# Seven products instead of eight for pairs of channel tiles, one shared work area, and low parts made by adding transfers

## The chip, the cores and the metric

The kernel runs on one core of a Trainium2 chip. The metric is device time in microseconds (us). The kernel before took 606.78 us, the median of three runs (606.14 to 609.61). The profile comes from one execution of 606.02 us, whose span from the first to the last instruction is 604.0 us.

The engines are TensorE (PE, matrix products; PEld is its weight load), VectorE (DVE), ScalarE (ACT), GpSimd (POOL) and SyncE (SP, which only issues transfers). Each works its own queue in order.

## The reference, cut to what matters

One layer of a hybrid backbone is applied to 128 context tokens and 512 latent tokens. All 640 tokens share one input projection of 1024 x 6176 weights. Its columns feed two head groups whose outputs are joined by a 2048 x 1024 output projection.

```python
h = _rms(x, norm_pre_w) * (1 + scale) + shift        # 640 tokens x 1024
u = h @ w_in
z, xbc, dt_raw, q, k, v, g = split(u)                # 1024, 2048, 32, 512, 512, 1024, 1024 columns
xbc = silu(depthwise_conv3(xbc) + conv_b)            # xs 1024, B 512, C 512
y_s = bidirectional_scan(C, B * dt, xs, decay) + D_skip * xs        # SSD, 16 heads, chunks of 128
y_s = _rms(y_s * silu(z), ssd_norm_w)
y_r = bidirectional_scan(rope(q), rope(k), v, fixed decay)          # retention, 8 heads
y_r = groupnorm(y_r) * ret_norm_w * silu(g)
out = concat([y_s, y_r]) @ w_out
y = x + gate * _rms(out, norm_post_w)
```

The convolution runs over neighbouring tokens, separately in context and latent tokens. So xs, B, C and z are wanted with channels on partitions and tokens along the row ("channel tiles" of 128 channels x 640 tokens). V, G, Q and K are wanted with tokens on partitions.

## The kernel before, in words

Every large product is made in three passes: each fp32 operand is split into a high part (rounded to the fp32r type) and a low part (the rest), and high x high, high x low and low x high are added in PSUM. `hh` and `hl` hold the two parts of the normalised input, eight k-tiles of 128 rows by 640 tokens.

Weights come in pieces of 256 KB (128 x 512 values), in the order that `plan` lists. `load_split` (L157) gives each a `raw` buffer (4 of them), a `whi` and a `wlo` buffer (7 each). SP loads `raw`, ACT rounds it into `whi` (L174), and VectorE subtracts to get `wlo` (through the helper `tt`, L131). `feed` (L181) keeps loads up to six pieces and splits up to three pieces ahead of use; `take` hands pieces to a product.

The kernel has a start phase, four stages g = 0 to 3, and the output projection:

- Start: for each k-tile, the modulation (tiles `mod`), transposes (`tr`), ScalarE's scaling into `h32`, the split into `hh`/`hl`, and the V and G columns of stage 0 into five accumulators `acc`. The order is written out by hand in the string `START`.
- A stage runs four kinds of products. `gemm_wide` makes V and G: 512 columns wide, all five token tiles open at once, k-tile by k-tile (tile `gw`; stage 0 has its V and G from the start phase). `gemm_tok` makes Q and K: 256 or 288 columns, token tile by token tile (tile `gt`). `gemm_z` makes the two z tiles of the stage before, and `gemm_s` makes B, C and two xs tiles. Both call `gemm_ch` (tile `gc`): one channel tile is 8 k-tiles x 3 passes x 2 halves of 320 tokens = 48 matmuls in two accumulators. `ev_conv` copies the result into `u` with ScalarE and does the convolution and SiLU; `ev_z` does the SiLU of z.
- Scan work is cut into small steps that are called between matmuls. `slot()` counts positions in the product code (66 in a full stage) and calls the steps that are due: `s_steps(g)` is the SSD scan of four heads, `r_steps(p)` the retention scan of two heads, `dt_steps` the step sizes. The calls `s_job` and `job` name the first and last slot of each.
- Output: `gemm_wide` over the retention half for 2 x 512 columns, over the SSD half for 512 columns, then `gemm_out` (tile `go`) for the last 512 columns in 256-column groups, with the residual and store per token tile.

`job(...)` sets where steps stand in the program, and the framework orders each engine's queue from that when the kernel is built, with what is ready first: retention tables that are called at slot 12 stand at 44 us in the trace. PSUM has five banks for product accumulators (`pg`) and three for scan work (`pi`). Memory for stage work lies in pools: `rp` for retention, `sp_` for SSD.

Of the kernel before, what the change touches and what calls it, by code (L numbers as in the profile page):

```python
# [17 lines left out]
P = 128  # L18
D = 1024
KT = 8  # L20
T = 640
NCK = 5
# [13 lines left out]
CU, CL, CDU, CDL, CPOS, CONE, CS0, CS1, CTP = (  # L36
    0, 128, 256, 384, 512, 640, 768, 896, 1024)
CN = 1040
# [10 lines left out]
G6:34 G6:012 H7:4 F2 G7:012 G7:34  # L49
# [3 lines left out]
def plan():  # L53

    want = []
    for p in range(4):
        if p:
            vg = [(a + p * 256, a + p * 256 + 256) for a in (V0, G0)]
            want += [("w_in", [k], vg) for k in range(KT)]
        qk = [(Q0 + p * P, Q0 + (p + 1) * P), (K0 + p * P, K0 + (p + 1) * P)]  # L60
        if p == 0:
            qk.append((DT0, DT0 + 32))
        want += [("w_in", [2 * s, 2 * s + 1], qk) for s in range(4)]
        zc = [Z0 + q * 256 + e * P for q in ([p - 1] if p else []) for e in range(2)]
        sc = [B0 + p * P, C0 + p * P, XS0 + p * 256, XS0 + p * 256 + P]
        if p == 3:
            sc += [Z0 + 768, Z0 + 768 + P]
        for a in zc + sc:
            want += [("w_in", list(range(4 * s, 4 * s + 4)), [(a, a + P)]) for s in range(2)]
    for half, cb in ((1, 0), (1, 2), (0, 0)):  # L70
        want += [("w_out", [8 * half + k], [(cb * 256, cb * 256 + 512)]) for k in range(KT)]
    for cb in (2, 3):
        want += [("w_out", [2 * s, 2 * s + 1], [(cb * 256, cb * 256 + 256)]) for s in range(4)]
    return want

# [8 lines left out]
def constants():  # L84
# [5 lines left out]
        np.where(p < 64, i + 1, 128 - i), np.ones((P, P)),  # L90
        np.broadcast_to(p % 32 == 0, (P, P)), np.broadcast_to(p % 32 == 1, (P, P)),
        np.concatenate([np.broadcast_to(127 - j, (P, 8)), np.broadcast_to(j, (P, 8))], axis=1),
# [13 lines left out]
def body(ctx, tc, io):  # L106
# [15 lines left out]
    def mm(out, a, b, start, stop, big=False):  # L122
        r = pe.matmul(out, lhsT=a, rhs=b, start=start, stop=stop)  # L123
        if big:
            last["mm"] = getattr(r, "ins", r)
# [26 lines left out]

    hh = hp.tile([P, KT, T], F32R, name="hh")
    hl = hp.tile([P, KT, T], F32R, name="hl")
# [3 lines left out]
    at = np.cumsum([0] + [len(rows) * sum(b - a for a, b in ranges) for _, rows, ranges in want])  # L158

    def load_split(n):  # L160

        _, rows, ranges = want[n]
        nk, c = len(rows), sum(b - a for a, b in ranges)
        extra = n == len(want) - 1
        raw = wp.tile([P, nk, c], F32, tag="raw", name="raw", bufs=4)
        hi = (wx[0] if extra else wp).tile([P, nk, c], F32R, tag="whi", name="whi", bufs=1 if extra else 7)
        lo = (wx[0] if extra else wp).tile([P, nk, c], F32R, tag="wlo", name="wlo", bufs=1 if extra else 7)
        sp.dma_start(
            out=raw.rearrange("p k c -> p (k c)"),
            in_=io["ws"][P * int(at[n]):P * int(at[n + 1])].rearrange("(p x) -> p x", p=P),  # L170
        )

        def split():
            act.copy(hi, raw)  # L174
            tt(lo, raw, hi.bitcast(F32), ALU.subtract)
        return hi, lo, split

    wx = []
    state = {"ld": 0, "sp": 0, "use": 0}
    pieces = {}  # L180

    def feed(ahead_load=4, ahead_split=2):
        while state["ld"] < min(len(want), state["use"] + ahead_load):
            pieces[state["ld"]] = load_split(state["ld"])
            state["ld"] += 1
        while state["sp"] < min(state["ld"], state["use"] + ahead_split):
            pieces[state["sp"]][2]()
            state["sp"] += 1

    def take(n):  # L190

        feed(max(4, n), n)
        got = [pieces.pop(state["use"] + i)[:2] for i in range(n)]
        state["use"] += n
        return got
# [5 lines left out]
    def slot():  # L201
        feed(6, 3)
        clock["slot"] += 1
        while jobs and jobs[0][0] <= clock["slot"]:
            jobs.pop(0)[2]()
# [32 lines left out]
    rp = tc.alloc_tile_pool(name="rp", bufs=1, side="right")  # L238
    st_ = tc.alloc_tile_pool(name="st", bufs=1, side="right")


    xs_t = []
    wm_t, w0_t = {}, {}
# [6 lines left out]
    def load_w0(kt):  # L250
        raw = st_.tile([P, 512], F32, tag="raw0", name="raw0", bufs=3)
        sp.dma_start(out=raw, in_=io["w0"][kt])
        w0_t[kt] = raw
# [17 lines left out]
    junk = hl.rearrange("p k t -> p (k t)")[:, KT * T - D - 1:]  # L271
# [28 lines left out]
    w0 = {}  # L300

    def split0(kt):
        raw = w0_t.pop(kt)
        hi = st_.tile([P, 512], F32R, tag="w0h", name="w0h", bufs=3)
        lo = st_.tile([P, 512], F32R, tag="w0l", name="w0l", bufs=3)
        act.copy(hi, raw)
        tt(lo, raw, hi.bitcast(F32), ALU.subtract)
        w0[kt] = (hi, lo)

# [10 lines left out]
    def h_tile(kt, ts):  # L320
        ash = ash_t[kt]
        h32 = st_.tile([P, 512], F32, tag="h32", name="h32", bufs=3)[:, 0:len(ts) * P]
# [3 lines left out]
        for c, u in ((0, [t for t in ts if t == 0]), (1, [t for t in ts if t])):  # L326
            if u:
                q = slice((u[0] - ts[0]) * P, (u[-1] + 1 - ts[0]) * P)
                act.activation(h32[:, q], tr[:, q], AF.Identity,
                               bias=ash[:, c:c + 1], scale=ash[:, 2 + c:3 + c])  # L330
        q = slice(ts[0] * P, (ts[-1] + 1) * P)
        vec.tensor_copy(hh[:, kt, q], h32)
        r = tt(hl[:, kt, q], h32, hh[:, kt, q].bitcast(F32), ALU.subtract)
# [7 lines left out]
    def gemm0(kt, t):  # L341
        wh, wl = w0[kt]
        s = slice(t * P, (t + 1) * P)
        mm(acc[t], hh[:, kt, s], wh, kt == 0, False)
        mm(acc[t], hh[:, kt, s], wl, False, False)
        mm(acc[t], hl[:, kt, s], wh, False, kt == KT - 1)
# [3 lines left out]
        "M": load_wm, "W": load_w0, "L": load_x, "A": mod_a, "S": split0, "B": mod_b, "N": norm_x, "R": rest_x,  # L350
    }
    for op in START.split():
# [8 lines left out]
        elif op[0] == "F":  # L361
            feed(k, 0)
        elif op[0] == "C":
            sp.dma_start(out=cst, in_=io["cst"])
            sp.dma_start(out=rope, in_=io["rope"])
        else:
            steps[op[0]](k)
# [40 lines left out]
    for t in range(NCK):  # L408
        ev_v(0, t, acc[t][:, 0:256])
        ev_g(0, t, acc[t][:, 256:512])  # L410
    st_.release()

    sp_ = tc.alloc_tile_pool(name="sp", bufs=1, side="left")
    sqacc = sp_.tile([P, T], F32, name="sqacc")
    dtr = sp_.tile([P, NCK, 32], F32, tag="m", name="dtr", bufs=2)

    def gemm_tok(n, ev):
        ws = take(4)
        for t in range(NCK):
            ps = pg.tile([P, 512], F32, tag="g", name="gt")  # L420
            s = slice(t * P, (t + 1) * P)
            for kt in range(KT):
                wh, wl = ws[kt // 2]
                mm(ps[:, 0:n], hh[:, kt, s], wh[:, kt % 2], kt == 0, False)
                mm(ps[:, 0:n], hh[:, kt, s], wl[:, kt % 2], False, False)
                mm(ps[:, 0:n], hl[:, kt, s], wh[:, kt % 2], False, kt == KT - 1, big=True)
                if kt in (3, 7):
# [724 lines left out]
```

## Time and profile before

| | us |
|---|---|
| median of 3 runs | 606.78 |
| the profiled execution | 606.02 |
| its span | 604.0 |
| TensorE busy | 582.3 |
| VectorE busy | 418.1 |
| ScalarE busy | 337.4 |
| GpSimd busy | 31.3 |
| granted TensorE clock, mean | 0.993 |

The parts of the span, by the tile that TensorE writes: start 0 to 62.5 us; stage 0 Q/K to 78.5 and its B, C, xs to 122.3; stage 1 to 230.7; stage 2 with V/G 230.7 to 265.6, Q/K to 283.4, z, B, C, xs to 339.8; stage 3 with V/G and Q/K to 392.3 and z, B, C, xs, z to 469.7; output projection 469.7 to 597; the rest to 604.

In such rows an engine's busy time is the union of its instructions' spans. The rows of a line give the count, then the busy time of the group and the mean duration in ns of one, then the idle time ahead of them.

### The profile page before, as it was taken

What the parts mean: (1) busy time and instruction counts of PE and PEld (TensorE: products, weight loads), DVE (VectorE), ACT (ScalarE), POOL (GpSimd) and SP (SyncE); (2) the same over time, 40 slices, a digit from 0 to 9 for tenths busy, and PEclk for the clock granted to TensorE, in tenths of its full rate; (3) what the DMA queues carried; (4) which work ended last, traced back from release to release, by engine and by line L of the source; (5) the groups of instructions that cost most, each with busy time, mean ns of one, the idle gap of its engine ahead of it and who ended that gap; (6) DMA issues with size and microseconds to landing.
All of it is one profiled execution on the core that took longest, in us unless ns stands there. A gap on an engine that the chain in (4) does not pass through costs nothing.

```text
span 604.0 us, 10966 instructions
## 1 busy us (share of the span) xinstructions
PE 582.3 (96%) x3833; PEld 521.5 (86%) x3833; DVE 418.1 (69%) x942; ACT 337.4 (56%) x934; POOL 31.3 (5%) x112
## 2 busy tenths in 40 slices
PE   5899998999999999999999999999999999999995
PEld 3577998978999998889999888999999777788895
DVE  3657498855698866668897746798867866743665
ACT  5436255665667764465766646566755857262421
POOL 1000001200000010000011000000110000000010
PEclk9899999999999999999999999999999999999998
DMA  8694231553335633232554223354537777384033
GB/s 348 229 362 161 63 105 48 162 146 109 99 97 159 185 91 86 80 122 70 189 172 112 76 69 105 102 163 131 160 96 223 209 266 221 116 272 120 18 109 135
DMA packets 47638, 87.44 MB, mean 145 GB/s; under 512 B 5792, under 2 KB 18656, under 8 KB 46048
## 3 DMA queue, kind: packets, MB, share of 16 engines
q1 hardware_dynamic: 47296, 86.57, 45.2%
q8 instruction: 30, 0.49, 0.3%
q14 instruction: 24, 0.20, 0.1%
q10 hardware_dynamic: 288, 0.18, 0.1%
HBM read 75.03 MB, written 9.60 MB: 140 GB/s over the span
## 4 chain that ended last, share of the span: by engine, by line
PE 65%; DVE 13%; ACT 9%; DMA 6%; issue 5%; POOL 2%; SPq 0%; POOLq 0%; DVEq 0%; ACTq 0%
PE gw L123 24%; PE gc L123 11%; PE gt L123 9%; PE acc L123 5%; PE go L123 4%; DMA cf<-cumd 3%; PE ss L123 2%; PE mod L123 2%; DVE wlo L131 2%; DVE SC L128 2%; PE sfb L123 1%; PE ry L123 1%; POOL sm L131 1%; DVE yc L128 1%; ACT jk L733 1%
## 5 line engine op out<-in xcount | busy, mean ns | idle before, releaser
L131 DVE TENSOR_TENSOR wlo<-raw,whi 128x512 fp32r<-128x512 f32 (+1 forms) x120 | 82.2, 690 | 49.2 <-ACT whi L174 48.3
L174 ACT CAST whi<-raw 128x512 fp32r<-128x512 f32 (+1 forms) x120 | 73.6, 619 | 76.3 <-PE gw L123 46.1
L123 PE MATMUL gc<-hh,whi 128*128 128x320 f32 x384 | 96.7, 331 | 0.0
L123 PE MATMUL gc<-hl,whi 128*128 128x320 f32 x384 | 88.3, 310 | 0.0
L123 PE MATMUL gc<-hh,wlo 128*128 128x320 f32 x384 | 87.6, 309 | 0.0
L123 PEld LDWEIGHTS gc<-hh,whi 128*128 128x128 f32 x384 | 63.9, 189 | 1.1
L123 PEld LDWEIGHTS gc<-hl,whi 128*128 128x128 f32 x384 | 64.3, 188 | 0.1
L123 PEld LDWEIGHTS gc<-hh,wlo 128*128 128x128 f32 x384 | 64.1, 188 | 0.0
L123 PE MATMUL gw<-whi,hh 128*128 128x512 f32 x120 | 50.6, 421 | 0.8 <-ACT u L484 0.8
L123 PE MATMUL gw<-whi,hl 128*128 128x512 f32 x120 | 47.0, 392 | 0.0
L123 PE MATMUL gw<-wlo,hh 128*128 128x512 f32 x120 | 46.8, 390 | 0.0
L123 PE MATMUL gt<-whi,hh 128*128 128x256 f32 (+1 forms) x160 | 46.3, 289 | 0.0
L123 PE MATMUL gt<-wlo,hh 128*128 128x256 f32 (+1 forms) x160 | 45.7, 286 | 0.0
L123 PE MATMUL gt<-whi,hl 128*128 128x256 f32 (+1 forms) x160 | 45.7, 286 | 0.0
L862 ACT ACTIVATE m<-gu,dt 128x128 f32<-128x128 f32 x80 | 31.3, 391 | 16.5 <-DVE gu L131 14.6
L834 ACT ACTIVATE cf<-cf,dmc 128x128 f32<-128x128 f32 x80 | 26.5, 393 | 18.4 <-DMA cf<-cumd 18.4
L131 DVE TENSOR_TENSOR m<-m,cf 128x512 f32<-128x512 f32 x40 | 27.5, 689 | 8.8 <-ACT cf L863 8.2
L123 PE MATMUL gw<-whi,mrh 128*128 128x512 f32 x80 | 32.3, 404 | 0.0
L123 PE MATMUL gw<-wlo,mrh 128*128 128x512 f32 x80 | 31.2, 391 | 0.0
L123 PEld LDWEIGHTS gt<-whi,hh 128*128 128x128 f32 x160 | 30.5, 190 | 0.7 <-issue 0.5
L863 ACT ACTIVATE cf<-gu,dt 128x128 f32<-128x128 f32 x80 | 31.0, 387 | 0.0
L123 PE MATMUL gw<-whi,mrl 128*128 128x512 f32 x80 | 30.9, 391 | 0.0
(232 smaller groups left out, 1327.8 us busy)
## 6 DMA issues: line engine op xcount, KB each, us to landing
raw<-ws SPq DMA_DIRECT2D x116, 256.0 KB, 2.8
cf<-cumd SPq DMA_DIRECT2D x20, 512.0 KB, 4.2
wm<-wm SPq DMA_DIRECT2D x8, 1024.0 KB, 8.2
mraw<-mixd SPq DMA_DIRECT2D x16, 320.0 KB, 3.4
ef<-ecumd SPq DMA_DIRECT2D x32, 128.0 KB, 3.3
wg<-wg SPq DMA_DIRECT2D x4, 1024.0 KB, 5.9
x<-x SPq DMA_DIRECT2D x5, 512.0 KB, 7.3
mixd<-rmix SPq DMA_DIRECT2D x20, 128.0 KB, 2.7
```

The source lines that it names most:

```text
L123: r = pe.matmul(out, lhsT=a, rhs=b, start=start, stop=stop)
L128: eng.scalar_tensor_tensor(out=out, in0=in0, scalar=s, in1=in1, op0=op0, op1=op1)
L131: return eng.tensor_tensor(out=out, in0=a, in1=b, op=op)
L174: act.copy(hi, raw)
L733: act.activation(jk, yc[:, h], AF.Square, scale=P ** -0.5, accum_out=sm[:, 2 + h:3 + h])
L834: act.activation(cf[:, e, 1, q], cf[:, e, 1, q], AF.Identity, bias=dmc[:, c, h:h + 1])
L862: act.activation(m[:, e, q], gu[:, 0], AF.Copy, scale=dt[:, c, h:h + 1])
L863: act.activation(cf[:, e, 1, q], gu[:, 1], AF.Copy, scale=dt[:, c, 16 + h:17 + h])
```

## The change

Pairs. `gemm_ch` becomes `gemm_pair`: two channel tiles (B and C, the two xs, the two z) form a 2 x 2 block product (two tiles x two halves of k, two halves of k x two halves of tokens). It is made of seven products of quarters in place of eight. Each product is 4 k-tiles x 3 passes = 12 matmuls of 322 columns, 84 for a pair where 96 stood. The token row gets two zero columns after the context and two at the end (`TW` = 644), so a half is 322. The seven results are combined in three accumulators X, Y, Z, two of them added to twice or kept open after a partial read, with ScalarE copies and five VectorE instructions of 322 columns:

```python
steps = [
    (X, half(0, 0), True, lambda: act.copy(s1, X)),
    (Y, sm(0), True, lambda: tt(b0, Y, s1, ALU.add)),
    (Z, sm(3), True, None),
    (Y, sm(1), False, lambda: (tt(b1, Y, s1, ALU.add), tt(b1, Z, b1, ALU.subtract))),
    (X, half(0, 4), False, lambda: act.copy(a0, X)),
    (Y, half(1, 4), False, lambda: tt(a1, Y, s1, ALU.add)),
    (Z, sm(2), False, lambda: tt(b0, Z, b0, ALU.subtract)),
]
```

The sums of input quarters `sh`, `sl` are made once in the start phase by `sums(k)`, for k = 0 to 3: four VectorE instructions of 322 columns, then for two rows of 644 a ScalarE copy and a VectorE subtraction. `START` calls three of them as T0, T1, T2; the fourth stands after the evacuation of `acc`.

```diff
-G6:34 G6:012 H7:4 F2 G7:012 G7:34
+T0 G6:34 G6:012 T1 H7:4 F2 G7:012 T2 G7:34
...
+    def sums(k):
+        a, b, c, d = (rows[k + i][:, h * HW:(h + 1) * HW] for i in (0, 4) for h in range(2))
+        tt(d, b, d, ALU.subtract)
+        tt(b, a, b, ALU.subtract)
+        tt(a, d, a, ALU.subtract)
+        tt(c, c, a, ALU.add)
+        for i in range(2):
+            r = rows.pop(k + 4 * i)
...
+            act.copy(hi, r)
+            tt(lo, r, hi.bitcast(F32), ALU.subtract)
```

Weight pieces. A pair has seven pieces where it had four in all: three quarters as they are, two sums of two quarters that POOL makes by an adding transfer onto a loaded quarter, and two sums that VectorE adds from neighbouring pieces. The buffers are 6 `raw` and 5 `whi`/`wlo`, loads stand up to six pieces past the last split, splits up to four ahead of use. Pieces of one k-tile of w_in (V/G of stages 1 to 3, Q/K of stage 0) get their low part another way: ScalarE writes minus the high part, and a POOL transfer adds the weights from memory onto it.

```diff
+    def pair(a, b):
+        lo, hi = list(range(4)), list(range(4, 8))
+        a11, a12, a21, a22 = (("w_in", k, [(c, c + P)]) for c in (a, b) for k in (lo, hi))
+        load(*a11)
+        want.append(("sum", (-1, 2)))
+        load(*a11, a21)
+        load(*a21, a22)
+        load(*a12)
+        want.append(("sum", (-4, -1)))
+        load(*a22)
...
+            if i:
+                pool.dma_start(out=out, in_=source(n, i), accum_op=ALU.add)
+            else:
+                sp.dma_start(out=out, in_=source(n, i))
...
+        if want[n][0] == "load" and want[n][1][0][0] == "w_in" and raw.shape[1] == 1 and n >= KT:
+            act.activation(lo, hi.bitcast(F32), AF.Copy, scale=-1.0)
+            pool.dma_start(out=lo.rearrange("p k c -> p (k c)"), in_=source(n, 0), accum_op=ALU.add)
+        else:
             tt(lo, raw, hi.bitcast(F32), ALU.subtract)
```

Shared work area. The tiles of the retention job move from `rp` to a pool `rw`, those of the SSD job from `sp_` to a pool `sw`. Both are opened at the same place and closed by the last step of their job, so that the two jobs follow one another. The slots follow suit:

```diff
-    job(dt_steps(), 11, 24.5)
-    job(r_steps(0), 10, 33)
+    job(dt_steps(), 10.5, 22)
+    job(r_steps(0), 12, 33)
...
-        s_job(g - 1, n + 2.5, n + 43.5, n + 51.75)
+        a, b = s_steps(g - 1)
+        job(a, n + 1, n + 36)
         gemm_r(g)
-        job(r_steps(g), n + 31.25, n + 67.25)
+        job(r_steps(g), n + 37, n + 65.5)
         gemm_z(g - 1)
+        job(b, n + 42.5, n + 43.5)
         gemm_s(g)
```

Smaller edits. Q/K go through `gemm_wide` (all five token tiles open, evacuated together at the end). The SSD result is added to D times xs chunk by chunk in `c2` (two more VectorE instructions of 128 columns per chunk), and `fin` loses its four (two of 512, two of 128 columns in a stage). z is evacuated with one ScalarE and one VectorE instruction of 644 columns per tile. `gemm_out` makes four token tiles 512 columns wide and the last in two groups of 256, and its eight weight pieces lie in the place of the retention half's input.

## Rows read from the trace of the kernel before

**Rows 1.** The page, part 1: busy us, share of the span, instructions.
```profile
PE 582.3 (96%) x3833; PEld 521.5 (86%) x3833; DVE 418.1 (69%) x942; ACT 337.4 (56%) x934; POOL 31.3 (5%) x112
```

**Rows 2.** Stretches: us, then busy us of PE, PEld, DVE, ACT, POOL; clock, DMA.
```profile
13.00:62.50 49.50, 47.09 (x302) 33.24 (x300) 32.07 (x91) 25.64 (x58) 1.91 (x3) 0.97 0.71 255
62.50:78.50 16.00, 16.00 (x122) 15.95 (x121) 7.53 (x24) 4.41 (x14) 0.27 (x6) 1.00 0.13 33
78.50:122.30 43.80, 41.27 (x291) 39.69 (x290) 37.85 (x108) 25.00 (x83) 6.55 (x19) 1.00 0.38 114
...
230.70:265.60 34.90, 34.34 (x167) 28.44 (x166) 20.11 (x38) 17.30 (x44) 0.41 (x4) 1.00 0.32 93
265.60:283.40 17.80, 17.80 (x157) 17.46 (x156) 13.25 (x37) 10.34 (x33) 0.00 (x0) 1.00 0.26 83
283.40:339.80 56.40, 56.00 (x409) 54.75 (x408) 46.97 (x98) 39.51 (x120) 5.30 (x19) 1.00 0.47 142
...
392.30:469.70 77.40, 76.55 (x546) 74.59 (x544) 61.80 (x128) 50.35 (x147) 5.32 (x16) 1.00 0.51 157
```

**Rows 3.** The first 33.6 us of a z, B, C, xs part, same columns.
```profile
283.40:317.00 33.60, 33.20 (x248) 32.07 (x247) 30.34 (x68) 24.25 (x77) 2.04 (x4) 1.00 0.54 173
```

**Rows 4.** Timeline of TensorE, 320 columns: start us, us, instruction; eight starts between.
```profile
302.68 0.45 PE L123 MATMUL gc<-hl,whi 128*128 128x320 f32 x2
...
303.85 0.46 PE L123 MATMUL gc<-hh,wlo 128*128 128x320 f32 x2
```

**Rows 5.** Timeline of TensorE, 512 columns: fifteen starts between.
```profile
130.03 0.39 PE L123 MATMUL gw<-whi,hl 128*128 128x512 f32 x1
...
133.43 0.39 PE L123 MATMUL gw<-whi,hl 128*128 128x512 f32 x1
```

**Rows 6.** Timeline of TensorE, 256 columns: nineteen starts between.
```profile
265.72 0.28 PE L123 MATMUL gt<-whi,hh 128*128 128x256 f32 x1
...
267.99 0.28 PE L123 MATMUL gt<-wlo,hh 128*128 128x256 f32 x1
```

**Rows 7.** VectorE's groups by shape in stage 2, 230.7 to 339.8 us.
```profile
L131 DVE TENSOR_TENSOR wlo<-raw,whi 128x512 fp32r<-128x512 f32 x24 | 16.4, 688 | 8.3 <-ACT whi L174 8.2
L131 DVE TENSOR_TENSOR m<-m,cf 128x512 f32<-128x512 f32 x10 | 6.9, 690 | 2.0 <-ACT cf L863 1.8
...
L128 DVE SCALAR_TENSOR_TENSOR xs<-u,cw,xs 128x641 f32<-128x641 f32 x4 | 3.5, 886 | 1.8 <-ACT xs L486 1.7
...
L128 DVE SCALAR_TENSOR_TENSOR zg<-zth,gc 128x320 f32<-128x320 f32 x4 | 1.8, 484 | 0.3 <-ACT zth L498 0.3
...
L131 DVE TENSOR_TENSOR ta<-gt,rope 128x256 f32<-128x256 f32 x4 | 1.7, 423 | 1.5 <-PE gt L123 1.5
...
L128 DVE SCALAR_TENSOR_TENSOR xs<-cth,xs 128x641 f32<-128x641 f32 x2 | 1.6, 824 | 0.2 <-ACT cth L490 0.2
...
L128 DVE SCALAR_TENSOR_TENSOR y<-xs,pk,y 128x512 f32<-128x512 f32 x2 | 1.4, 750 | 0.0
...
L131 DVE TENSOR_TENSOR rk<-ta,tb 128x128 f32<-128x128 f32 x4 | 1.1, 285 | 0.0
...
L128 DVE SCALAR_TENSOR_TENSOR y<-xs,pk,y 128x128 f32<-128x128 f32 x2 | 0.7, 345 | 0.0
...
L884 DVE COPY y<-sy 128x256 f32<-128x256 f32 x1 | 0.4, 424 | 0.3 <-PE sy L123 0.3
```

**Rows 8.** ScalarE's split in the same stage.
```profile
L174 ACT CAST whi<-raw 128x512 fp32r<-128x512 f32 x24 | 14.7, 616 | 14.9 <-PE gw L123 8.3 <-PE gt L123 4.3 <-PE gc L123 2.0
```

**Rows 9.** Timeline: two VectorE instructions on end, and a GpSimd power.
```profile
304.76 0.89 DVE L128 SCALAR_TENSOR_TENSOR zg<-zth,gc 128x320 f32<-128x320 f32 x2
...
304.96 0.71 POOL L131 TENSOR_TENSOR sm<-sm,mhalf 128x2 f32<-128x2 f32 x1
```

**Rows 10.** Weight loads, line 168: issue to landing.
```profile
DMA to landing us min/median/max: 2.4/2.8/8.8
```

**Rows 11.** Waits of VectorE: us in total, times, longest.
```profile
DVE yc L128 <- POOL sm L131: 18.5, 17, 1.8
```

More of the change, by code (lines that the diff above doesn't have):

```diff
@@ L21 @@
 T = 640
+TW = 644
+HW = 322
 NCK = 5
@@ L70, in plan @@
[L70 to L73, printed above, removed]
-    return want
+            for k in range(KT):
+                load("w_in", [k], qk + [(DT0, DT0 + 32)])
+        else:
+            for k in range(0, KT, 2):
+                load("w_in", [k, k + 1], qk)
+            pair(Z0 + (p - 1) * 256, Z0 + (p - 1) * 256 + P)
@@ new lines, in plan, with sources @@
+        pair(B0 + p * P, C0 + p * P)
+        pair(XS0 + p * 256, XS0 + p * 256 + P)
+    pair(Z0 + 768, Z0 + 768 + P)
+    for half, cb in ((1, 0), (1, 2), (0, 0), (0, 2)):
+        for k in range(KT):
+            load("w_out", [8 * half + k], [(cb * 256, cb * 256 + 512)])
+    return want
+def sources():
+    at, size, order = {}, 0, []
+    for kind, of in plan():
+        for m, rows, cols in of if kind == "load" else ():
+            key = (m, tuple(rows), tuple(cols))
+            if key not in at:
+                at[key] = size
+                size += len(rows) * sum(b - a for a, b in cols)
+                order.append((m, rows, cols))
+    return at, size, order
@@ L151, in pkc @@
         return pk[:, base + n:base + n + 1]
[L153 to L154 removed]
+    hh = hp.tile([P, KT, TW], F32R, name="hh")
+    hl = hp.tile([P, KT, TW], F32R, name="hl")
     want = plan()
[L158 to L174, printed above, removed]
[L175 to L176 removed]
@@ L178, in body, with source @@
[L178 to L184, printed above, removed]
+    where = sources()[0]
+    state = {"ld": 0, "sp": 0, "use": 0}
+    pieces, split_of, late = {}, {}, {}
+    def source(n, i):
+        m, rows, cols = want[n][1][i]
+        a = P * where[m, tuple(rows), tuple(cols)]
+        size = P * len(rows) * sum(b - a for a, b in cols)
+        return io["ws"][a:a + size].rearrange("(p x) -> p x", p=P)
@@ new lines, in load @@
+    def load(n):
+        kind, of = want[n]
+        nk, c = (4, P) if kind == "sum" else (len(of[0][1]), sum(b - a for a, b in of[0][2]))
+        raw = pieces[n] = wp.tile([P, nk, c], F32, tag="raw", name="raw", bufs=6)
+        for i in range(len(of) if kind == "load" else 0):
+            out = raw.rearrange("p k c -> p (k c)")
+            if i:
+                pool.dma_start(out=out, in_=source(n, i), accum_op=ALU.add)
+            else:
+                sp.dma_start(out=out, in_=source(n, i))
@@ L185, in feed @@
+    def feed():
+        first = len(want) - KT
+        while state["ld"] < min(len(want), state["sp"] + 6, state["use"] + 10):
+            load(state["ld"])
             state["ld"] += 1
-        while state["sp"] < min(state["ld"], state["use"] + ahead_split):
-            pieces[state["sp"]][2]()
+        while state["sp"] < min(first, state["ld"], state["use"] + 4):
+            split(state["sp"])
             state["sp"] += 1
[L190 to L195, printed above, removed]
+        if state["use"] > first - KT and first <= state["sp"] < state["ld"]:
+            split(state["sp"])
+            state["sp"] += 1
@@ L410, in body @@
         ev_g(0, t, acc[t][:, 256:512])
+    sums(3)
     st_.release()
+    state["use"] = KT
+    for n in range(KT):
+        pieces.pop(n)
+        split_of.pop(n)
     sp_ = tc.alloc_tile_pool(name="sp", bufs=1, side="left")
[L414 to L427, printed above, removed]
-                    if kt == 7:
-                        ev(t, ps)
-                    slot()
```

417 lines of the change are left out of this document (229 added, 188 removed).

## The prediction

> **What bounds the kernel now.** I read the totals first. TensorE is busy for 582.3 of 604.0 us, VectorE for 418.1, ScalarE for 337.4 [rows 1]. Then the stretches, part by part [rows 2]: from the end of the start phase on TensorE is nearly full in every part, so the time is TensorE's stream plus small gaps. VectorE is not even. It works 33.4 of 52.7 us while V/G and Q/K run, but 47.0 of 56.4 us while z, B, C and xs run, and 30.3 of 33.6 us in the first piece of that part, with TensorE idle for 0.4 us there [rows 3]. That is the row to keep in mind: the change takes work from TensorE and gives work to VectorE where VectorE has least room. Last the spacing of matmuls on the timeline, which says what one costs in a stream: 1.17 us over 8 starts or 146.3 ns at 320 columns [rows 4], 226.7 ns at 512 [rows 5], 119.5 ns at 256 with a single accumulator [rows 6]. The mean durations on the page are about twice that, because matmuls overlap.
>
> **TensorE, part by part.** Between 320 and 512 columns a column costs 0.42 ns, so 322 columns cost 147.1 ns. Before: 24 tiles x 48 = 1152 matmuls x 146.3 ns = 168.5 us. After: 12 pairs x 84 = 1008 x 147.1 ns = 148.3 us. The gain is 20.2 us. One accumulator in a row, as in the new products, costs nothing by [rows 6], which lie on the same line of time over columns. The last product goes from 240 x 119.5 ns = 28.7 us to 96 x 226.7 + 48 x 119.5 ns = 27.5 us, a gain of 1.2. Q/K keep their matmuls. So TensorE's stream gets 21.4 us shorter, and the profiled 606.0 us would become 584.6.
>
> The Trainium skill (TensorE: Matmul & The Clock Gate, section Back-to-back issue gap) gives columns / 2.4 + 2.5 ns, which would be an estimate of 135.8 and 136.7 ns and a gain of 18.6 in place of 20.2. The rows show some 10 ns more for each matmul, so the rows are used.
>
> **VectorE's new work.** For a pair: five evacuations of 322 columns, nearest row 0.484 us for 320 from PSUM, 2.4; two sums of pieces at 0.688, 1.4; three more low parts (seven where there were four) at 0.688, 2.1. Together 5.9 us, against 1.7 us that TensorE saves on it [rows 7]. In a stage, adding to D times xs chunk by chunk costs 10 x 0.345 - 2 x 0.750 - 2 x 0.345 - 0.424 = +0.8, and z in one piece 2 x 0.824 - 4 x 0.484 = -0.3 [rows 7]. The low parts that go to transfers take off 8 x 0.688 = 5.5 a stage, but in V/G.
>
> Now the z, B, C, xs part of stage 2. Start from 47.0. Three pairs add 17.6; the two small edits 0.5. The SSD job had 13.5 of its 41 slots there and has 6 of 35 now: its ten groups, from m to the copy of y, sum to 26.3 us [rows 7], so 4.2 go. Q/K are evacuated at the end in place of tile by tile: four groups, ta to rk, sum to 5.9 [rows 7], three of four tiles move in, +4.4. The second xs tile is finished only with its pair, so its convolution (2 x 0.886 + 0.824 = 2.6) moves out. That is 62.7 us. Instructions on end overlap by 0.08 us (two take 0.89, not 0.97 [rows 9]); about half of some 130 do already, so a full queue may save 5 more: 58 to 63 us of VectorE for 56.4 - 5.1 = 51.3 us of TensorE. The V/G and Q/K part gets 33.4 - 5.5 + 4.2 - 4.4 + 2.6 = 30.3 for 52.7. A stage as a whole fits (93 of 104 us); the part does not, by 7 to 12.
>
> The same for stage 0 after its Q/K: 37.9 + 2 x 5.9 + 4.4 - 2.6 = 51.4, or 47 on end, for 43.8 - 3.4 = 40.4: over by 7 to 11. Stage 3 with four pairs: 61.8 + 23.4 + 0.2 - 4.2 + 4.4 = 85.6, or 79 on end, for 77.4 - 6.8 = 70.6: over by 8 to 15. With stage 1 as stage 2, four parts are over by 29 to 50 us in all.
>
> What does TensorE lose? Nothing at the least, if job work slips behind what it waits for and into the next V/G, which has 22 us free. At the most all but the 1.8 us (12 x 147 ns) after which accumulator Y is wanted again, 4 x 1.8 off, 43 us. I take 2 us a part, 8 in all, near the low end: the instructions that TensorE itself waits for (15 evacuations, 21 low parts, 6 sums: 25.8 us) are half of the part, splits stand four pieces or 7.1 us ahead, and the nearest row shows VectorE at 90% with TensorE at 99% [rows 3].
>
> **Start.** Each of the four sums costs VectorE 4 x 0.484 + 2 x 0.824 = 3.6 us [rows 7], 14.3 in all. Two must end before a buffer for rows 6 and 7 is free, where VectorE works 32.1 of 49.5 us; the others fall on Q/K with 8.5 us free and 3 us of low parts gone [rows 2]. Bounds 0 and 7 (two chains wholly open); I take 2.
>
> **Q/K with five accumulators at once.** TensorE meets the fifth after 15 matmuls of V/G, 3.4 us; ten evacuations of 256 columns at 0.42 (nearest row, the copy of y [rows 7]) are 4.2. Bounds 0 and 2 each time; 0.5 x 4 = 2.
>
> **Adding transfers.** There are 24 for pairs and 32 for low parts, on POOL's queue. No row has one. The nearest is the weight load, 2.4 to 8.8 us to landing with a median of 2.8 [rows 10], and 0.7 us of POOL as for its power [rows 9]. A low part of V/G then takes 2 x 0.616 [rows 8] + 0.7 + 2.8 = 4.7 us, with four pieces of 1.77 us as a lead, 7.1: hidden, and 3.6 us late at 8.8. A sum in a pair takes 2.8 + 0.7 + 2.8 = 6.3 from a free buffer, has three pieces or 5.3 us and then the lead: hidden, and 5.9 late with 8.8 twice. I take 0. Behind a POOL transfer that waits for its load stand the powers of the retention job, for which VectorE waits 18.5 us already [rows 11].
>
> The Trainium skill (DMA: Bandwidth & Descriptors, section Anatomy of one DMA) prices a GpSimd-issued transfer at 2.0 us plus bytes over 436 GB/s, an estimate of 2.6 us for 256 KB. By that the third rival below falls away. No run here shows it yet.
>
> **ScalarE.** Nine more high parts and eight negated ones a stage at 0.616 are 10.5 us, less about 2 for the copies of the convolution; 67.2 of 109.1 us becomes 76 of 104 [rows 2, 8]. It has room; without it splits come late as with VectorE.
>
> **Sum.** 606.0 - 21.4 + 8 + 2 + 2 = 596.6. The profiled run lies 0.8 below the median, so 597.
>
> **Rivals.**
> - *All of it slips.* TensorE loses only the start's 2: 587. For it: a stage as a whole has VectorE at 90%. Against: the SSD job must end before the retention job may open the shared area, so jobs can slip only in turn.
> - *VectorE sets the pace of the z, B, C, xs parts* (the other side). Its queue is served in order, and what jobs put ahead of an evacuation delays it. If TensorE gets by for two products (3.5 us) and then waits, with the middle of each overload: 9 - 3.5, twice 9.3 - 3.5, 11.5 - 3.5, or 25 us; 584.6 + 25 + 4 = 613. It decides once VectorE needs over 55 us in a part of 51. For it: 58 to 63; waits behind POOL would add to that. Against: [rows 3].
> - *Adding transfers land late*, at about 8 us: V/G of three stages starts near 3 us late, 8 in all on top of the forecast: 605. For it: transfers took 8.8 at worst [rows 10]. Against: those were in the start, with the DMA busy for 0.71 of the time; later it is 0.26 to 0.51 [rows 2].
>
> **Numbers.** A difference under 0.5% (3 us) cannot be told from none. Chances: forecast 0.36 (own range 591 to 603), all slips 0.18, VectorE's pace 0.29 (606 to 622), late transfers 0.17 (600 to 610). Faster than 603.7: 0.34 + 0.18 + 0.06 = 0.58. Slower than 609.8: 0.25 + 0.02 = 0.27. Between: 0.15. The range 585 to 614 leaves out little below and less than half of the second rival above.
>
> **What would show it.** 1008 matmuls of 322 columns at 147 ns prove the gain. VectorE near 58 us and TensorE's gaps near 2 us in z, B, C, xs of stage 2 fit the forecast; gaps of 6 us or more with VectorE above 95%, ended by VectorE ahead of the products, mean the second rival; gaps ahead of the first V/G matmuls ended by a POOL transfer mean the third. I am wrong on the mechanism if the gaps lie elsewhere, in the start or where the shared area changes hands.

## The result and the profile after

The changed kernel takes 656.23 us, the median of three executions (654.74 to 661.90), against 606.75 for the kernel before: a ratio of 1.083 (95% interval 1.074 to 1.092). One execution of 1137 us, and one of 659.04 us in the run with sums on GpSimd below, were in another, slower state and are left out of every figure (counting the first, the median above would be the 659 from which the expectations below start). The forecast of 597 was some 60 us too low, and its range (585 to 614) does not hold the time. The profiled execution took 661.9 us, with a span of 660.0.

First the page: busy time of each engine, then busy tenths and the granted clock in 40 slices, then the chain that ended last.

```profile
PE 595.0 (90%) x3593; PEld 513.8 (78%) x3593; DVE 468.3 (71%) x1059; ACT 372.8 (56%) x974; POOL 81.7 (12%) x144
...
PE   5899897988899898898998899999898799999995
...
DVE  4459578955579995465799846679999986755354
...
PEclk9699997999999998898998999999899899999998
...
PE 46%; DMA 19%; DVE 14%; ACT 13%; issue 5%; SPq 1%; POOL 1%; DVEq 0%; POOLq 0%; ACTq 0%
```

TensorE has 240 matmuls fewer than in [rows 1] and yet more busy time, and is busy for 90% in place of 96%. The clock is below full speed in many slices: 47.8 us of the span at the lower level of 1.2 GHz (besides the end), where before there were 3.4 us. Transfers hold 19% of the chain; before it was 6%.

The stream itself is as forecast. On the timeline of TensorE (start us, us, instruction) eleven starts of 322 columns take 1.62 us at full clock, 147.3 ns each (forecast 147.1); seven starts at the lower clock take 1.88 us, 269 ns each. Here are the first and the last start of each kind:

```profile
256.57 0.47 PE L154 MATMUL gc<-hh,whi 128*128 128x322 f32 x1
...
258.45 0.47 PE L154 MATMUL gc<-sl,whi 128*128 128x322 f32 x1
...
515.26 0.31 PE L154 MATMUL gc<-sh,whi 128*128 128x322 f32 x1
...
516.88 0.31 PE L154 MATMUL gc<-sh,wlo 128*128 128x322 f32 x1
```

What was lost stands in the waits of TensorE: engine and line, what it waited for, us in total, times, longest.

```profile
PE gc L154 <- DVE u L162: 8.6, 3, 3.1
PE gw L154 <- DMA wlo<-ws: 7.8, 3, 2.8
...
PE gw L154 <- DVE rzg L159: 4.8, 3, 2.1
PE gw L154 <- ACT mrh L1108: 3.9, 1, 3.9
PE st L876 <- ACT tok L877: 3.6, 2, 2.2
PE cums L154 <- DVE s L162: 3.1, 1, 3.1
```

I added up the times between starts of all matmuls, as a budget of the span (before to after): big products at their spacing of [rows 4 to 6], 448.7 to 427.5 us; gaps between instructions, 14.0 to 55.9; at the lower clock what the big products take over that spacing and all that the scan's matmuls take (more than the clock alone costs), 2.6 to 29.1; the scan's matmuls at full clock and small delays in the stream, 130.8 to 138.2. So a gain of 21.2 stands against 76 of losses; the difference is 55 of the 56 us by which the span grew. A dozen gaps of 1.6 to 3.9 us, past the first 25 us, make 32 of these, and beside ten of the twelve a stretch at 1.2 GHz begins within 2 us.

Two of these waits on the timelines, first VectorE and then TensorE about 228 us:

```profile
226.79 0.69 DVE L162 TENSOR_TENSOR wlo<-raw,whi 128x512 fp32r<-128x512 f32 x1
227.59 0.83 DVE L162 TENSOR_TENSOR sqacc<-sqacc,u 128x644 f32<-128x644 f32 x1
228.34 0.48 DVE L162 TENSOR_TENSOR u<-gc,s 128x322 f32<-128x322 f32 x1
...
226.09 0.31 PE L154 MATMUL gc<-hh,wlo 128*128 128x322 f32 x1
228.88 0.64 PE L154 MATMUL gc<-sh,whi 128*128 128x322 f32 x1 [2.48 <-DVE u L162]
```

Then ScalarE, GpSimd and TensorE about 252 us:

```profile
245.35 0.60 ACT L227 CAST whi<-raw 128x512 fp32r<-128x512 f32 x1
247.14 0.62 ACT L227 CAST whi<-raw 128x512 fp32r<-128x512 f32 x1 [1.18 <-PE gc L154]
...
249.08 1.15 ACT L229 ACTIVATE wlo<-whi 128x512 fp32r<-128x512 f32 x2
...
249.37 0.71 POOL L162 TENSOR_TENSOR sm<-sm,mhalf 128x2 f32<-128x2 f32 x1
250.04 1.84 POOL L230 DMA_DIRECT2D wlo<-ws  x2
...
254.66 0.47 PE L154 MATMUL gw<-wlo,hh 128*128 128x512 f32 x1 [2.83 <-DMA wlo<-ws]
254.96 0.31 PE L154 MATMUL gc<-hh,whi 128*128 128x322 f32 x1
```

In the first, VectorE works down `fin` (its last instruction is the sum of squares) ahead of the evacuation of Y, and TensorE wants Y again. In the second, the roundings are those of the first two pieces of V/G in stage 2. The adding transfer for the first low part stands behind a power of the retention job on GpSimd's queue, takes 0.9 us to issue, and lands at 254.52, 4.48 us after its start. The 24 matmuls of the pair's last two products stand behind that V/G matmul in TensorE's queue, and run from 254.96 on without a wait. How long transfers take, from the page's part 6 (count, KB each, us to landing):

```profile
raw<-ws SPq DMA_DIRECT2D x136, 256.0 KB, 3.3
...
raw<-ws POOLq DMA_DIRECT2D x24, 256.0 KB, 4.5
wlo<-ws POOLq DMA_DIRECT2D x24, 256.0 KB, 5.5
mraw<-mixd SPq DMA_DIRECT2D x16, 320.0 KB, 5.6
```

### The profile page after: what moved, and what is told of

Its sections match the earlier page's. It is cut to its first block, busy times and chain, and to the rows that moved or that the text cites. A ratio compares the mean times of both kernels' runs of the same rounds, so it can differ in the third digit from the quotient of the medians.

```text
span 660.0 us, 10877 instructions
## 1 busy us (share of the span) xinstructions
PE 595.0 (90%) x3593; PEld 513.8 (78%) x3593; DVE 468.3 (71%) x1059; ACT 372.8 (56%) x974; POOL 81.7 (12%) x144
## 4 chain that ended last, share of the span: by engine, by line
PE 46%; DMA 19%; DVE 14%; ACT 13%; issue 5%; SPq 1%; POOL 1%; DVEq 0%; POOLq 0%; ACTq 0%
PE gw L154 14%; PE gc L154 13%; DMA cf<-cumd 9%; PE acc L154 4%; PE go L154 3%; ACT cf L931 2%; DMA ef<-ecumd 2%; DMA wlo<-ws 2%; PE mod L154 2%; DMA mixd<-rmix 2%; ACT cf L960 2%; DMA mraw<-mixd 2%; ACT m L959 2%; PE ry L154 2%; DVE wlo L162 2%
## 5 line engine op out<-in xcount | busy, mean ns | idle before, releaser
L162 DVE TENSOR_TENSOR wlo<-raw,whi 128x512 fp32r<-128x512 f32 x128 | 87.6, 686 | 23.3 <-ACT whi L227 23.2
L154 PE MATMUL gw<-whi,hh 128*128 128x512 f32 (+2 forms) x280 | 98.4, 357 | 5.2 <-DVE rzg L159 4.8
L154 PE MATMUL gw<-wlo,hh 128*128 128x512 f32 (+2 forms) x280 | 95.0, 340 | 7.8 <-DMA wlo<-ws 7.8
L154 PE MATMUL gw<-whi,hl 128*128 128x512 f32 (+2 forms) x280 | 94.7, 339 | 0.0
L154 PE MATMUL gc<-sh,whi 128*128 128x322 f32 x192 | 66.0, 344 | 8.8 <-DVE u L162 8.6
L154 PEld LDWEIGHTS gw<-wlo,hh 128*128 128x128 f32 x280 | 54.5, 195 | 13.0 <-issue 5.6
L154 PEld LDWEIGHTS gw<-whi,hh 128*128 128x128 f32 x280 | 53.9, 195 | 11.9 <-DVE rzg L159 5.4
L154 PE MATMUL gc<-sl,whi 128*128 128x322 f32 x192 | 62.6, 326 | 0.0
L154 PE MATMUL gc<-sh,wlo 128*128 128x322 f32 x192 | 62.0, 323 | 0.0
L154 PEld LDWEIGHTS gw<-whi,hl 128*128 128x128 f32 x280 | 54.3, 194 | 5.2
L154 PE MATMUL gc<-hh,wlo 128*128 128x322 f32 x144 | 47.8, 332 | 0.7 <-DVE wlo L162 0.7
```

What stands on the lines that cost most here:

```text
L154: r = pe.matmul(out, lhsT=a, rhs=b, start=start, stop=stop, skip_group_check=again)
L162: return eng.tensor_tensor(out=out, in0=a, in1=b, op=op)
```

## The experiments

Times are medians; each is followed by its ratio to the kernel before on the same chip and its 95% interval. The kernel before took 606.8 to 609.7 us (medians) from chip to chip, so differences between two kernels are taken from their ratios (0.001 is 0.61 us); under some 3 us they cannot be told from none. Since runs of one kernel differ in their granted clock, a second number helps: over all kernels here, one more us at 1.2 GHz (2 x (1 - mean clock) x span) goes, between runs of the same kernel, with 0.36 us more time. This is a fit over 98 executions, not an experiment; where a time is called "at full clock", it is the mean span less 0.36 times the mean time at 1.2 GHz, an estimate. By that the 43.7 us of the changed kernel (mean of three runs) against 8 to 10 before cost about 12 us, and at full clock its span would be 640 against 603.

**no_add.** Low parts by VectorE again.
```diff
-        if want[n][0] == "load" and want[n][1][0][0] == "w_in" and raw.shape[1] == 1 and n >= KT:
-            act.activation(lo, hi.bitcast(F32), AF.Copy, scale=-1.0)
-            pool.dma_start(out=lo.rearrange("p k c -> p (k c)"), in_=source(n, 0), accum_op=ALU.add)
-        else:
-            tt(lo, raw, hi.bitcast(F32), ALU.subtract)
+        tt(lo, raw, hi.bitcast(F32), ALU.subtract)
```


> The low part of every one-k-tile piece is a VectorE subtraction again (as before the change); the pairs and their products stay. Theory A (late hand-overs and the clock that falls after them make the time): the three TensorE waits that end on a transfer into wlo (7.8 us of gaps at 80, 254 and 379 us) and the half clock behind each (three stretches of 3.4 us, some 1.7 us lost in each) go: 659 falls to 644 to 650. Theory B (VectorE sets the pace, as the prediction's second rival said): some 72 subtractions of about 0.75 us, 54 us, come back onto VectorE, and the time does not fall, 659 to 680. Theory C (the adding transfers as such are innocent, their gaps are replaced by others at the same places): 655 to 662.


640.54 us, 1.057 (1.051 to 1.063): 15.8 less and 3 below theory A's range, with VectorE busier (482.5 us). The waits for `wlo<-ws` are gone, those for `u` are the same. Putting work back onto the busier engine was right here; theory B falls for these pieces (it also counted 72 subtractions, 54 us; there are 32, and VectorE's busy time grew by 14). The edit takes away three things at once: the transfers, ScalarE's negated copies and GpSimd's time to issue.

**fin_late.**
```diff
-        job(b, n + 42.5, n + 43.5)
+        job(b, n + 46.5, n + 50.5)
```


> Only the last steps of the state-space part of each group (y*z, the square and its sum) are queued 4 and 7 slots later, behind the evacuations of the first pair. Theory A: the three gaps in front of the z pair's second product (2.5 + 3.1 + 3.1 = 8.6 us, all ended by a VectorE evacuation) go, and with them the three stretches at half clock: 659 falls to 645 to 652. Theory B (VectorE is simply full there): the same waits turn up a few slots later, 655 to 662.


652.66, 1.075 (1.070 to 1.080): 4.9 less, with intervals that overlap, and by the fit all of it clock (at full clock 640, as before the edit). The 8.6 us for `u` went, and this came instead, VectorE late in small portions:
```profile
PE gw L154 <- DMA wlo<-ws: 8.7, 3, 3.0
PE gw L154 <- DVE rzg L159: 6.0, 3, 2.7
...
PE gc L154 <- DVE wlo L162: 3.2, 7, 0.9
```
So both theories hold in part: the named waits went, as theory A said, but the time lies between the two ranges.

**eight.** `gemm_pair` makes two tiles of eight products with ScalarE evacuation; four pieces for a pair, no sums of weights or inputs.
```diff
-        load(*a11)
-        want.append(("sum", (-1, 2)))
...
+        for q in (a11, a12, a21, a22):
+            load(*q)
...
+                        mm(ps[h], a[:, kt % 4], b[:, kt, h * HW:(h + 1) * HW], kt == 0 and n == 0,
+                           kt == KT - 1 and n == 2, big=True)
...
+                act.copy(u[:, 1 + h * HW:1 + (h + 1) * HW], ps[h])
```


> The pairs are undone: each pair of channel tiles is again two tiles of eight products each, with no sums of weights or of inputs and ScalarE evacuation; the shared work area, the adding transfers and the new order of the output product stay. TensorE's stream is some 20 us longer than after the change. Theory A (the gaps belong to hand-overs at three kinds of place, and only one of them is in the pairs): the gaps at V/G that end on a transfer (7.8 us) and those at ScalarE's copies (about 8 us) stay, those in the pairs (8.6 us) go: 645 to 660, still well above 607. Theory B (the pairs' VectorE load is the whole cause): all gaps and all stretches at half clock go, and the time is 605 to 618.


627.56, 1.032 (1.026 to 1.038), between the ranges of the two theories. So the pairs cost 31 us in all, though TensorE's stream is 20 us shorter with them. Without pairs no wait for an adding transfer is left among the large ones, which theory A did not expect. The first low part of V/G in stage 2 still takes 7.3 us from rounding to landing (9.2 in the changed kernel), but it starts much earlier: 19.3 us ahead of its matmul, where the changed kernel has 6.5 (245.35 to 251.83). A piece of the two tiles lasts for 24 matmuls where a piece of a pair lasts for 12, so the same four pieces of lead are twice as long; and here V/G of that stage stands behind all products of the tiles.
```profile
218.89 0.62 ACT L222 CAST whi<-raw 128x512 fp32r<-128x512 f32 x1 [0.66 <-PE gc L149]
...
238.18 0.39 PE L149 MATMUL gw<-wlo,hh 128*128 128x512 f32 x1
```
Waits for ScalarE's copies are left:
```profile
PE st L855 <- ACT tok L856: 4.7, 3, 2.3
PE ss L149 <- ACT tok L856: 2.5, 1, 2.5
PE gw L149 <- DVE rzg L154: 2.3, 2, 1.6
```

**fill.** Ten products that nothing reads ahead of the fourth step of the z pair, and ten ahead of V/G, in three groups.
```diff
+        for _ in range(n):
+            mm(ps, hh[:, 0, 0:P], hh[:, 0, 0:512], True, True)
```


> Adds 10 products of 512 columns that nothing reads ahead of the fourth step of the z pair and ahead of V/G in three groups, where the longest gaps stand: 60 products, 13.6 us at the 226.7 ns of a 512-column product, some of it inside gaps of 2.2 to 3.1 us (six gaps, 15.5 us). Theory A (the half clock that follows a gap costs time of its own): the half-clock stretches behind those gaps (228, 255, 303, 354, 379, 471 us; 1.7 us lost in each) go, and the filling stands in the place of the gaps: the time is between 8 us shorter and no change, 648 to 659, in spite of 13.6 us more work. Theory B (the clock is a bystander): 659 to 673.


658.46, 1.083 (1.076 to 1.089). Inconclusive: no change of the ratio in spite of 13.6 us more work, as theory A allows, but the lower clock did not go (51.2 us); gaps shrank by 10 us and new ones came elsewhere (ScalarE's `tok`, 6.7 us).

**stall_long, stall_short.** The kernel before with stalls in eight tiles; the products after a stall are held by `tc.issue_after`.
```diff
+    def stall():
+        ps = pg.tile([P, 512], F32, tag="g", name="gs")
+        mm(ps[:, 0:2], ident, tick[:, 0:2], True, True)
+        act.copy(tick[:, 2:4], ps[:, 0:2])
...
+        mm(ps[:, 2:4], ident, tick[:, 4:6], True, True, big=True)
```
What is left out are eight small GpSimd operations in a row, of the long stalls alone.

> The kernel before, with eight stalls put into the first z and the first xs tile of each group: TensorE, a ScalarE copy, eight small GpSimd operations in a row, TensorE again, and nothing of the tile may pass. Each should leave TensorE idle for some 2.5 to 3 us, 20 to 24 us in all. Theory A (a gap of this length also brings the granted clock down behind it): stretches at half clock behind most of the eight, some 1.7 us lost in each, so the time grows by the gaps and 10 to 14 us more: 607 becomes 637 to 645. Theory B (only the idle time counts): the clock stays up, 624 to 632.

> The kernel before, with 32 stalls of a ScalarE copy alone (four in each of the eight tiles), some 0.5 to 0.7 us each, 16 to 22 us in all. Both theories: no stretch at half clock behind them, and the time grows by the idle time alone: 607 becomes 620 to 630. If half clock follows these too, its cause is the sum of idle time in a stretch and not the length of one gap.


633.93, 1.043 (1.037 to 1.048), and 626.35, 1.031 (1.027 to 1.035). The long stalls came out at 1.6 to 2.2 us (first row of waits). Of the 32 short ones only six left TensorE idle (second row); the others were mostly filled with scan products.
```profile
PE gs L123 <- POOL tick L476: 15.1, 8, 2.2
...
PE gs L123 <- ACT tick L468: 2.4, 6, 0.7
```
So the two runs do not have the same idle time, and the difference between them (7.2 us) does not price the clock: of the 21.6 us by which the span of the short stalls is longer than that of the kernel before, 12.3 are the stalls' own small products, 7.0 scan products and 1.5 idle time. That short gaps leave the clock alone was not tested. What the long stalls show is that gaps bring the clock down: mean time at 1.2 GHz was 25.0 us with them, 9.7 with the short stalls and 8.0 in the kernel before on that chip. The 17 us more would be worth 6 us at 0.36, so that a gap costs more than its length; this price is an estimate. In the profiled execution two of the eight gaps were followed by stretches at 1.2 GHz, one of 6.8 and one of 3.4 us, so "most of the eight" was wrong there; but it was the fastest of the four, and the others spent 25 to 29 us at 1.2 GHz in place of its 18.

**area_alone, area_apart.** The frame of the change: eight and no_add together, with `gemm_tok` for Q/K of stages 1 to 3. Then the same with separate areas for the jobs, as the diff shows.
```diff
-            rw[0] = tc.alloc_tile_pool(name="rw", bufs=1, side="left")
+            rw[0] = RW
...
-            sw[0] = tc.alloc_tile_pool(name="sw", bufs=1, side="left")
+            sw[0] = SW
```


> Of the change only the shared work area, the new deadlines of the jobs, rows of 644 columns and the order of the last product are left: no pairs (two tiles of eight products each), low parts by VectorE, Q/K of stages 1 to 3 token tile by token tile. TensorE's stream is that of before. Theory A (the shared area delays its first broadcasts: ScalarE and its copies stand behind them, as in the run without pairs, where three gaps of 1.6 to 2.5 us were ended by ScalarE's tok copies or VectorE's rzg, with three stretches at half clock): 615 to 624, some 8 to 15 us over before. Theory B (what was left of the loss in the run without pairs came from adding transfers and Q/K): 605 to 611.

> As the run with the shared area alone (618.6), but the two jobs have their own areas again, as before the change, and the buffers for the sums of the input are gone. Theory A (the shared area, whose transfers can start only when the other job has let go, costs the 12 us): 606 to 611. Theory B (the cost lies in the rest of the frame: rows of 644 columns, the new order of pieces and splits, the deadlines): 615 to 620.


618.56, 1.018 (1.014 to 1.022), and 618.57, 1.017 (1.014 to 1.021). The first came out where theory A had it, but for another reason: of the waits that theory A named it shows one, of 0.6 us, and the second shows that sharing the area costs nothing without pairs. The other edits of the frame cost 11 us. In the trace of the second these are thin: 2.3 us in the start, 0.9 to 2.6 in each V/G, 1.9 in one z, B, C, xs part, 1 in stage 0, and 1 in the output, where `gemm_out` was to save 1.2. Which edit makes them stays open.

**two_fixes, three_fixes.** no_add with fin_late; then Q/K of stages 1 to 3 by `gemm_tok` as well.
```diff
-        gemm_wide(hh, hl, lambda t, ps: ev_qk(p, t, ps), off, *((288, 1) if p == 0 else (256, 2)))
+        if p == 0:
+            gemm_wide(hh, hl, lambda t, ps: ev_qk(p, t, ps), off, 288, 1)
+        else:
+            gemm_tok(256, lambda t, ps: ev_qk(p, t, ps))
```


> Low parts by VectorE again and the last steps of the state-space job queued later, both at once. Theory A (the two hold-ups are at different places and add): 659 - 18.5 - 6.5, 630 to 637. Theory B (with both gone VectorE is the one that is late: 54 us of subtractions and all evacuations in its queue): 637 to 645, with more gaps ended by VectorE than in either run alone.

> Low parts by VectorE, the last steps of the state-space job later, and Q/K of stages 1 to 3 token tile by token tile as before the change. In the run with two fixes Q/K began with a gap of 3.0, 1.6 and 1.5 us in the three stages, ended by VectorE's evacuation of V/G, because five accumulators at once need all five PSUM buffers. Theory A (that need is the cause): these gaps go, 638 becomes 631 to 634. Theory B (VectorE is behind anyway and is met a little later): 636 to 640.


638.31, 1.054 (1.047 to 1.061), and 637.38, 1.046 (1.039 to 1.052). Whether the two costs add cannot be told: fin_late brings 4.9 us alone and 1.6 on top of no_add, with a spread of some 3 on each. The time is theory B's. The wait at Q/K is this row with two fixes:
```profile
PE gw L154 <- DVE rzg L159: 6.1, 3, 3.0
```
It is gone with three, as theory A said, but the time is theory B's: 1 us less by the medians, 5 by the ratios and 4 at full clock, with intervals that overlap. VectorE is met later instead; waits of three_fixes:
```profile
PE sy L154 <- DVE m L162: 6.3, 5, 2.3
...
PE gc L154 <- DVE wlo L162: 4.5, 7, 1.4
PE gw L154 <- ACT mrh L1122: 3.3, 1, 3.3
```

**three_fixes_gpsimd_sums.**
```diff
-                tt(pieces[m], x, y, ALU.add)
+                tt(pieces[m], x, y, ALU.add, eng=pool)
```


> On top of the three fixes the 24 sums of weight pieces go from VectorE to GpSimd: 24 x 0.69 = 16.5 us less for VectorE, in its fullest parts. Theory A (VectorE's queue sets the pace of the pairs): 8 to 16 us less than with three fixes, unless GpSimd needs over 2 us for one. Theory B (the loss is in hand-overs and transfers): no change within 3 us.


650.95, 1.066 (1.059 to 1.074): 13 more, outside both theories. A sum took GpSimd 1.36 us where VectorE took 0.69, in a queue with transfers and powers, and TensorE waited 16.1 us for `whi`. VectorE's own instruction `cf` went from a mean of 687 ns in three_fixes to 841: three of the twenty, each begun 0.1 us after a sum on GpSimd, took 1.72 us, the others 0.68 to 0.69. The two groups by line (count, busy us, mean ns, idle before):
```profile
L162 POOL TENSOR_TENSOR raw<-raw 128x512 f32<-128x512 f32 x24 | 32.6, 1360 | 82.8 <-DVE wlo L162 36.6 <-issue 16.6 <-DMA raw<-ws 10.9
...
L162 DVE TENSOR_TENSOR cf<-cf 128x512 f32<-128x512 f32 x20 | 16.8, 841 | 8.1 <-ACT cf L945 8.1
```

**three_fixes_light_pairs, three_fixes_plain_loads, light_and_plain.** Bounds for what the pairs ask of VectorE and of adding transfers. The first leaves out VectorE's sums of pieces and the combining of the seven results (ScalarE copies stand there), the second the second operand of the other sums, the third both.
```diff
-            (Y, sm(0), True, lambda: tt(b0, Y, s1, ALU.add)),
+            (Y, sm(0), True, lambda: act.copy(b0, Y)),
...
-                tt(pieces[m], x, y, ALU.add)
+                sp.dma_start(out=pieces[m].rearrange("p k c -> p (k c)"), in_=source(m - 1, 0))
```
```diff
-        for i in range(len(of) if kind == "load" else 0):
+        for i in range(1 if kind == "load" else 0):
```


> On top of the three fixes VectorE is freed of what the pairs gave it: the sums of weight pieces are replaced by plain loads of another piece, and the evacuations that add or subtract are ScalarE copies (the outputs of the pairs are then not the sums that they should be; products, splits and order stay). VectorE has 12 x (5 x 0.48 + 2 x 0.69) = 45 us less, ScalarE some 21 us more. Theory A (VectorE's overload in the pairs is what keeps the gain of 21 us from showing): 595 to 610. Theory B (transfers, the shared area and the start keep it): 622 to 634.

> On top of the three fixes the 24 adding transfers of the pairs are left out: the pieces that should be differences hold one operand only. VectorE's work stays. Theory A (VectorE's pace): no change within 4 us. Theory B (the adding transfers, 4.5 us to landing and queued behind their loads on GpSimd, come late in the pairs as they did in V/G): 8 us less or more than that.

> On top of the three fixes (637) both at once: VectorE freed of the pairs' work (623.6 alone) and the pairs' adding transfers left out (625.9 alone); the outputs of the pairs are then not the sums that they should be. Theory A (VectorE's load and the adding transfers are two separate costs): 610 to 615. Theory B (both delay the same splits, so that one of them is enough): 621 to 626. Theory C (together they were all that kept the gain from showing): 586 to 598.


623.56, 1.022 (1.016 to 1.029); 625.89, 1.028 (1.023 to 1.033); together 608.30, 1.001 (0.999 to 1.003; the kernel before took 609.7 on the chip of the first two, 607.9 on that of the third). VectorE's work in the pairs is worth 14.1 us alone and 16.3 with plain loads; the adding transfers 10.6 alone and 12.7 with light pairs; both together 26.9. Within 3 us they are separate costs that add; theory A comes nearest, the time 2 us below its range. Even with both gone the time is that of the kernel before. Busy times of light_and_plain:
```profile
PE 571.7 (95%) x3593; PEld 499.4 (83%) x3593; DVE 445.8 (74%) x1007; ACT 371.9 (62%) x990; POOL 34.8 (6%) x88
```
Its longest wait of TensorE after the start:
```profile
PE gw L154 <- ACT mrh L1122: 4.5, 1, 4.5
```
Its parts say where the stream's gain went: the parts with pairs are 0.4, 2.9, 4.5 and 1.1 us shorter than before in stages 0 to 3, where the matmuls alone would give 3.4, 5.1, 5.1 and 6.8 (the last holds that wait of 4.5 us); the start is 2.7 us longer and V/G in three stages 1.6, 1.1 and 0.9. No version here beats the kernel before.

## Why the prediction was wrong, step by step

Put in one line, from the ratios in the order in which the edits were taken off: 606.8 - 21.2 (stream) + 10.9 (frame) + 15.8 (low parts) + 1.6 (`fin`) + 5.2 (Q/K) + 26.9 (VectorE's work and adding transfers in the pairs) = 646.0, and 11 us up to the 657.0 of the ratio that no run prices. The terms for `fin` and Q/K are within the noise. For the 11 us there are readings only: with light pairs and plain loads the first output product still waits 4.5 us, since `mraw` now lies where the sums of the input lay and loads only after the last pair (its first load is issued at 461.14 us, 1 us after that pair's last product starts; in the kernel before it was 450.2); and 20.5 us at 1.2 GHz in place of 8, worth 4.5 us by the fit.

- *TensorE stream, -21.4*: right, 147.3 ns and -21.2. The 1.2 of it for the last product was not seen in the time.
- *Adding transfers, 0*: the step that failed most, 15.8 and 10.6 us. The forecast took 4.7 us for a low part, with 2.8 us to landing from SP's loads, and 7.1 us of lead. The transfers took 4.5 and 5.2 to land (the estimate of 2.6 beside the forecast was lower still), and the way to the first piece of V/G in stage 2 was 9.2 us: rounding at 245.35; the negated copy at 249.08, behind the rounding of the second piece, which waited 1.18 us for a buffer that TensorE still read, and six more instructions in ScalarE's queue; issue at 250.04, landing at 254.52. TensorE wanted it at 251.83, so the lead was 6.5 us. That is so early because the order fixed when the kernel is built has this matmul ahead of the pair's last two products; that another order would hide the transfer is likely from the trace but was not run. The third rival had the kind of wait, with 8 us in V/G of three stages; the waits were 7.8 us at Q/K of stage 0 and at V/G of stages 2 and 3, and its 8.8 us for one transfer were never reached (at most 8.3). It left out that a gap brings the clock down, and that the copies queue on ScalarE.
- *VectorE's overload, 2 us a part, 8 in all*: too small, 14 to 16. But VectorE did not run at 95% with gaps of 6 us, as the second rival had it. In the z, B, C, xs part of stage 2, which the prediction's signs name, it was busy for 53.5 of 62.1 us where 58 to 63 of 51 were forecast (fourth line below, columns as in [rows 2]); V/G and Q/K before it had 36.4 us of VectorE's work (second and third line) where 30.3 were forecast, so jobs did slip. TensorE was idle for 6.2 us of that part, 5.7 of them in two gaps: one for `u`, one for an adding transfer. Stage 1 is alike (first line; the first products of the next V/G lie among its last), and only stage 3 came to 77.6 of 82.8 (last line). TensorE lost time not where VectorE was full on average but where an instruction it needed stood behind others: `fin`, evacuations, low parts.
```profile
197.90:260.20 62.30, 55.86 (x363) 52.54 (x361) 52.20 (x128) 36.18 (x96) 11.60 (x17) 0.95 0.57 137
260.20:299.50 39.30, 36.78 (x179) 29.66 (x177) 24.29 (x44) 25.26 (x66) 5.18 (x6) 0.96 0.74 178
299.50:322.40 22.90, 19.58 (x157) 18.86 (x155) 12.14 (x24) 13.82 (x43) 1.75 (x2) 0.93 0.23 73
322.40:384.50 62.10, 55.87 (x359) 52.38 (x360) 53.45 (x130) 36.25 (x96) 10.29 (x16) 0.95 0.55 134
...
439.80:522.60 82.80, 73.28 (x481) 68.53 (x479) 77.57 (x173) 52.63 (x135) 10.77 (x15) 0.98 0.57 151
```
- *Q/K with five accumulators, 0.5 each, bounds 0 and 2*: the gaps were 1.7, 2.1 and 1.0 us in stages 1 to 3, over the value taken; the one of 2.1 passed its bound. Taking them off brought 1 to 5 us, within the noise.
- *Start +2, ScalarE has room*: the start is 5 us longer in the profiled run, and 10.2 us of it went at 1.2 GHz against 3.4. ScalarE has room on average, but its in-order queue held the copies `tok`, the `th` for which VectorE's `rzg` waited (7.3 us in three waits), and the negated copies.
- *Left out altogether*: the frame, 11 us, as a sum of many edits that had each been put at nothing; and the clock, 12 us by the fit over runs, which is no further term of the line above but a share of its terms. A term for the clock was missing although [rows 2] show 0.97 in the start, the one part with long gaps.

By its own list of signs, "I am wrong on the mechanism if the gaps lie elsewhere" came true for four of the twelve large gaps: two at ScalarE's `tok`, one at the step sizes of stage 0 (`s`, 3.1 us), one at the output's first load. Six lie where the second and the third rival looked (`u` and the adding transfers), two at Q/K.

## What to carry to other kernels

Where one engine is busy for 96% and the others serve it, price an edit by what each queue holds ahead of the instruction that the busy engine needs next, place by place; an engine's share of a stretch did not show it here. A transfer in place of an instruction brings its landing and every queue on its way into the lead, so take the landing from a row with the same issuing engine, or allow twice the nearest. And a gap on TensorE is to be counted with what follows it: here some 0.36 us, by the fit, for each us at the lower clock.

## What the runs showed of the hardware

Adding transfers from GpSimd's queue took 0.86 to 0.88 us to issue (median) and 4.5 (24 onto loaded weights) or 5.2 us (all 32 onto negated copies) to land, at most 8.3. The Trainium skill (SBUF — State Buffer, section SBUF: two separate sides) warns that such a transfer can wait for its descriptors while VectorE runs an instruction in a mode that takes the port pair it shares with GpSimd. The trace gives no sign of such a wait: of the 32 onto negated copies, the half with VectorE busier in the first 3 us after the issue landed after 4.4 us in the mean, the other half after 6.4. More transfers in flight go with later landing: the half with more of them in these 3 us landed after 6.3, the other after 4.6. This is a count over one trace, and no run varies the one without the other.

In that section the Trainium skill also says that VectorE and GpSimd hold the shared port pair in turn, a VectorE instruction with two inputs in SBUF against a GpSimd one that reads SBUF: who starts first keeps it for the whole instruction. The run with sums on GpSimd agrees. Three `cf` minima on VectorE, each begun 0.1 us after a sum on GpSimd, took 1.72 us and ended 0.5 us after it, where the other seventeen took 0.68 to 0.69. Five sums on GpSimd that began during VectorE's instruction `m` took 1.65 to 1.78 us, the other nineteen 1.25 to 1.30.
